# The first expert's rows by fp32 products with the residual, not by a gather

## The chip, the cores and the metric

One Trainium2 chip, one of its cores. The metric is the time of the whole program on the device in microseconds; three runs of the kernel are shown by their median. Engines are named as in the profile: PE is TensorE (PEld its weight loads), DVE VectorE, ACT ScalarE, POOL GpSimd, SP the engine that only issues transfers.

## The reference, cut to what matters

The program runs two transformer layers and then a second block, whose last part is a mixture of 16 experts over 512 tokens of 1024 features:

```python
h = rms_norm_2(x, ffn_norm_gain[i])        # x * rsqrt(mean(x*x) + eps) * gain
x = x + hierarchical_moe(h, ...)

# hierarchical_moe: 4 groups of 4 experts, top-2 experts inside the best group
gates = sum(one_hot(e_glob, N_EXPERTS) * weights[..., None], axis=1)
a = einsum('td,edf->tef', ht, w_e_gate)
u = einsum('td,edf->tef', ht, w_e_up)
hid = silu(a) * u * gates[:, :, None]
out = hid.reshape(t, N_EXPERTS * D_EXPERT) @ w_e_down.reshape(...)   # D_EXPERT = 256
```

## The kernel before

All big products are made of three fp32r products (a high part and a low part of each side, `mm3` and `mm3s`), so each weight tile of 128x2048 is split into a high part on ACT and a low part on DVE before use (`split`, L2004; `whi`, `wlo`).

The class `Moe` does the last part. For each of the four tiles of 128 tokens, `row` (from L1821) transposes the residual `X[t]`, forms the router's logits with eight fp32 products of 20 columns (L1838), gets the norm's factor r by a power on POOL (`rsqrt`, L278), writes the normalised rows `h` to a DRAM tensor `h_rows` (L1841) and the residual to the output (L1842). `route` then picks two experts for each token and gives every chosen token a place, a rank, among the rows of its expert: `rank` (L1892) is a 128x8 tile, one column for each of two choices and four token tiles. `placed` compares the ranks with the slot numbers 0 to 127 (L1899) and sums with small bf16 products (L1909) a table `tab` (L1910): for each expert a list of 128 token numbers, with a number past the end in empty slots. The same is done for the gate weights, `wts`.

`finish` runs 19 slots in order, 16 experts and 3 extra ones for experts with more than 128 tokens. For each slot `gather` (L1977) fetches the 128 rows from `h_rows` by an indirect transfer on POOL's queue into one of three tiles XE, which are the residual tiles `X[0]` to `X[2]`, filled with zeros first (L2071). `rows_in` transposes the rows on PE (L1992), and splits them into a high part on ACT (L1993) and a low part on DVE (L1994), both out of one PSUM tile of two banks. `hidden` makes 24 products with the gate and up weights (L252 to L254), with the next slot's `rows_in` called between its two halves (`between`), then the activation on ACT and the product with the gate weight on DVE (L2024, L2025). `turn` transposes the result (L2032), and `down` multiplies it with the down weights (L260 to L264) and adds the rows to the output by an indirect transfer (L2048). `down` of a slot follows `hidden` of the next one.

Weights come over SP's queue into a ring of 13 buffers (`fetch`, L1811), two transfers in flight at a time; a buffer is free again once `split` has read it. One fetch, the one that is issued when 13 have been sent, also waits for the first gather (`self.first`).

Dependencies and the order of instructions on each engine come from a scheduler of the framework at build time, which follows the program's order as a priority, and takes what is ready by its own timeline. Each engine then works through its list in that order.

Of the kernel before, what the change touches and what calls it, by code (L numbers as in the profile page):

```python
# [10 lines left out]
F32 = mybir.dt.float32  # L11
F32R = mybir.dt.float32r
# [3 lines left out]
AF = mybir.ActivationFunctionType  # L16
ALU = mybir.AluOpType
AX = mybir.AxisListType
SP = mybir.EngineType.SP
P = 128  # L20
D = 1024
KC = 8
# [137 lines left out]
class Kern:  # L160
# [108 lines left out]
                                                                         mybir.DependencyReason.DATA),  # L269
                               reason="side by side")  # L270

    def rsqrt(self, ss, n, dim):

        v = self.nc.vector
        x, y, u = self.tiny(n), self.tiny(n), self.tiny(n)
        v.tensor_scalar(x, ss, 1.0 / dim, EPS, op0=ALU.mult, op1=ALU.add)
        if n <= 4:
            self.nc.gpsimd.tensor_tensor(y, x, self.mhalf[:, :n], op=ALU.pow)  # L278
            return y
        v.tensor_single_scalar(y.bitcast(I32), x.bitcast(I32), 1, op=ALU.logical_shift_right)  # L280
        v.tensor_scalar(y.bitcast(I32), y.bitcast(I32), -1.0, float(0x5F3759DF), op0=ALU.mult, op1=ALU.add)
        for _ in range(3):
            v.tensor_mul(u, y, y)
            v.scalar_tensor_tensor(u, u, -0.5, x, op0=ALU.mult, op1=ALU.mult)
            v.scalar_tensor_tensor(y, u, 1.5, y, op0=ALU.add, op1=ALU.mult)
        return y
# [1450 lines left out]
class Moe:  # L1737
# [4 lines left out]
    def __init__(self, K, out):  # L1742
        self.K, self.out = K, out
        nc, v, gp = K.nc, K.nc.vector, K.nc.gpsimd
# [32 lines left out]
        v.tensor_mul(self.wr, self.wr, K.sm("ffn_gain")[:, :, None].to_broadcast([P, KC, 20]))  # L1777
        self.gain = self.mp.tile([P, D], F32, tag="row", name="ffn_gain")
        nc.scalar.dma_start(self.gain, K.A["ffn_gain"][None, :].to_broadcast([P, D]))
        self.ring = []  # L1780
        self.order = [(0, 0), (0, 1)]
        for e in range(1, 16 + self.EXTRA):
# [12 lines left out]
    def one(self, name, shape, dt=F32):  # L1795
        return self.mp.tile(shape, dt, name=name)
# [24 lines left out]
    def row(self, x, t):  # L1821

        K = self.K
        nc, v = K.nc, K.nc.vector
        d = slice(t * P, t * P + P)
        xT = self.xp.tile([P, KC, P], F32R, tag="xl", name=K.nm("xT")).bitcast(F32)
        b = K.bank2().rearrange("p (k t) -> p k t", k=KC)
        for k in range(KC):
            nc.tensor.transpose(b[:, k, :], x[:, k * P:k * P + P], K.ident)
        for k in (slice(0, 4), slice(4, 8)):  # L1830
            self.turned = nc.scalar.copy(xT[:, k], b[:, k]).ins
        ss = K.tiny(1)
        h = self.xp.tile([P, KC, P], F32R, tag="xh", name=K.nm("h")).bitcast(F32).rearrange("p k t -> p (k t)")
        nc.scalar.activation(h, x, AF.Square, accum_out=ss)
        r = K.rsqrt(ss, 1, D)
        b = K.bank()
        for k in range(KC):
            nc.tensor.matmul(b[:, :20], xT[:, k, :], self.wr[:, k, :], start=k == 0, stop=k == KC - 1)  # L1838
        v.scalar_tensor_tensor(self.lg[:, t, :], b[:, :20], r, K.sm("r_bias"), op0=ALU.mult, op1=ALU.add)
        v.scalar_tensor_tensor(h, x, r, self.gain, op0=ALU.mult, op1=ALU.mult)  # L1840
        nc.gpsimd.dma_start(self.h_d[d, :], h)  # L1841
        nc.gpsimd.dma_start(self.out[d, :], x)  # L1842

    def route(self):
# [45 lines left out]
        tmp4 = tmp.rearrange("p (x t) e -> p x t e", x=2)  # L1890
        v.tensor_mul(tmp4, E4, b[:, :64].rearrange("p (x t e) -> p x t e", x=1, t=4).to_broadcast([P, 2, 4, 16]))
        v.tensor_reduce(rank, tmp, axis=AX.X, op=ALU.add)  # L1892
        cnt, kx, inc, ovb = (one(n, [P, 16]) for n in ("cnt", "kx", "inc", "ovb"))
        v.tensor_copy(cnt, b[:, 64:80])

# [78 lines left out]
    def gather(self, s, xe):  # L1974
# [4 lines left out]
        self.first = self.first or ins  # L1979
        return xe, at  # L1980

    def rows_in(self, pool, xe):

        K = self.K
        nc = K.nc
        if len(self.xs_) < 2:
            self.xs_.append(K.pair(self.xp, "x", [P, KC, P]))
        x = self.xs_[self.nx % 2]
        self.nx += 1
        b = K.bank2().rearrange("p (k t) -> p k t", k=KC)  # L1990
        for k in range(KC):
            nc.tensor.transpose(b[:, k, :], xe[:, k * P:k * P + P], K.ident)  # L1992
        nc.scalar.copy(x[0], b)  # L1993
        nc.vector.tensor_sub(x[1], b, x[0].bitcast(F32))  # L1994
        return x
# [55 lines left out]
    def finish(self, X):  # L2051
# [15 lines left out]
        for i in range(self.NA, self.NA + 5):  # L2067
            self.fetch(i)
        next(r)
        for x in XE:  # L2070
            nc.gpsimd.memset(x, 0.0)  # L2071
        tab = {s: self.gather(s, XE[s]) for s in range(A3)}
        for i in range(self.NA + 5, n1):
            self.fetch(i)
        regs = {}
# [12 lines left out]
            return get  # L2088

        next(r)  # L2090
        x = {0: self.rows_in(pool, tab[0][0])}
        g = {}
        for e in range(N + 1):
            if R <= e <= R + 3:
                next(r, None)
            if e < N:
                if e + A3 < N:
                    tab[e + A3] = self.gather(e + A3, XE[e % A3])

                def rows():  # L2100
                    x[e + 1] = self.rows_in(pool, tab[e + 1][0])
                g[e] = self.hidden(pool, x[e], unit(e), self.wts[:, e:e + 1], rows if e + 1 < N else None)
            if e:
                self.down(g[e - 1], unit(e - 1), Y[e % len(Y)], tab[e - 1][1])
            if e < N:
                g[e] = self.turn(pool, g[e])
# [41 lines left out]
```

## Time and profile before

| what | value |
|---|---|
| median of three runs | 2228.39 us |
| the runs | 2230.19, 2228.39, 2227.59 us |
| the profiled execution | 2229.89 us |
| its span | 2228.2 us |
| granted clock of TensorE, mean | 0.977 |
| PE busy | 2116.9 us |
| DVE busy | 1388.3 us |
| ACT busy | 970.8 us |

The profile is of one execution, and its times count from the start of the span. Busy is the sum of an engine's instructions; a wait is named by what released the engine. The granted clock is the share of 2.4 GHz that PE was given; 0.5 is 1.2 GHz.

### The profile page before, as it was taken

The numbers are of one execution on the slowest core, as the hardware profiler recorded it, in microseconds if no ns is written. First come the engines' busy times: TensorE is split into PE (matmuls) and PEld (weight loads), VectorE is DVE, ScalarE is ACT, GpSimd is POOL, SyncE is SP. The second block draws the span as 40 slices with busy tenths as digits, with TensorE's granted clock in tenths as the row PEclk, the third lists the DMA queues.
The fourth block names the chain that finished last, engine by engine and source line by source line (L and its number), as shares of the span: only waits on it lengthen the run. The fifth ranks groups of instructions, "written<-read, shape, count | busy, mean of one in ns | idle before, by whom it ended". The sixth has DMA issues, their size and how long they took to land. (4 is left out here: it accounts for less than half of the span.)

```text
span 2228.2 us, 28898 instructions
## 1 busy us (share of the span) xinstructions
PE 2116.9 (95%) x11224; PEld 1718.3 (77%) x11224; DVE 1388.3 (62%) x2420; ACT 970.8 (44%) x1484; POOL 327.4 (15%) x457
## 2 busy tenths in 40 slices
PE   6999999999999999999989999999989998997996
PEld 5976668888888888778877888888878875776875
DVE  3666664899744544551694588555646845747875
ACT  5446655521211211451553543222354545635865
POOL 0026632111000000330000100001130000012222
PEclk8999999999999999999999999999999998998998
DMA  7112231557511211121211133424323342668894
GB/s 296 58 38 77 97 142 46 175 186 253 179 58 57 76 57 57 39 92 57 78 57 39 55 110 114 151 91 141 114 92 115 129 143 89 219 256 275 297 307 131
DMA packets 54459, 281.11 MB, mean 126 GB/s; under 512 B 9200, under 2 KB 9600, under 8 KB 29360
## 3 DMA queue, kind: packets, MB, share of 16 engines
q1 hardware_dynamic: 33968, 219.39, 27.6%
q0 software_dynamic: 19344, 57.14, 8.4%
q10 hardware_dynamic: 1008, 2.70, 0.4%
q8 instruction: 90, 1.47, 0.3%
q14 instruction: 49, 0.40, 0.1%
HBM read 266.64 MB, written 26.18 MB: 131 GB/s over the span
## 5 line engine op out<-in xcount | busy, mean ns | idle before, releaser
L233 ACT CAST whi<-raw 128x2048 fp32r<-128x2048 f32 x106 | 202.5, 1911 | 588.9 <-PE b L264 382.8
L234 DVE TENSOR_TENSOR wlo<-raw,whi 128x2048 fp32r<-128x2048 f32 x106 | 246.1, 2323 | 219.4 <-ACT whi L233 217.7
L262 PE MATMUL b<-hl,whi 128*128 128x512 f32 (+1 forms) x736 | 283.2, 385 | 2.6 <-DVE t L335 1.6
L260 PE MATMUL b<-hl,whi 128*128 128x512 f32 (+1 forms) x736 | 282.9, 385 | 1.1 <-ACT whi L233 0.9
L264 PE MATMUL b<-hl,wlo 128*128 128x512 f32 (+1 forms) x736 | 280.5, 385 | 0.0
L833 DVE TENSOR_TENSOR acc<-acc,b 128x512 f32<-128x512 f32 x280 | 180.7, 682 | 147.7 <-PE b L264 147.6
L260 PE MATMUL b<-whi,hid 128*128 128x512 f32 x640 | 213.0, 391 | 3.0 <-ACT whi L233 1.9
L262 PE MATMUL b<-wlo,hid 128*128 128x512 f32 x640 | 214.3, 390 | 0.0
L264 PE MATMUL b<-whi,hid 128*128 128x512 f32 x640 | 211.7, 390 | 0.0
L262 PEld LDWEIGHTS b<-hl,whi 128*128 128x128 f32 x736 | 138.5, 188 | 30.7 <-issue 3.2
L264 PEld LDWEIGHTS b<-hl,wlo 128*128 128x128 f32 x736 | 138.6, 188 | 30.2 <-issue 2.0
L260 PEld LDWEIGHTS b<-hl,whi 128*128 128x128 f32 x736 | 138.4, 188 | 29.6 <-ACT whi L233 1.3
L2004 DVE TENSOR_TENSOR wlo<-raw,whi 128x2048 fp32r<-128x2048 f32 x57 | 129.8, 2288 | 30.8 <-ACT whi L2004 30.8
L260 PEld LDWEIGHTS b<-whi,hid 128*128 128x128 f32 x640 | 118.8, 188 | 27.5 <-ACT whi L233 2.1
L264 PEld LDWEIGHTS b<-whi,hid 128*128 128x128 f32 x640 | 120.1, 188 | 25.6
L262 PEld LDWEIGHTS b<-wlo,hid 128*128 128x128 f32 x640 | 120.1, 188 | 25.0
L2004 ACT CAST whi<-raw 128x2048 fp32r<-128x2048 f32 x57 | 108.2, 1912 | 10.1 <-PE b L254 10.1
L645 POOL TENSOR_TENSOR p<-p,t 128x512 f32<-128x512 f32 (+2 forms) x96 | 92.5, 972 | 63.7 <-DVE t L644 63.3
L414 DVE CUSTOM_DVE_ANT_0 junk<-mw,cb 128x1024 bf16<-128x1024 f32 x80 | 97.6, 1220 | 6.0 <-DMA mw<-in_w_modT_dram 5.4
L641 DVE CUSTOM_DVE_ANT_0 p<-b,mask,nsink 128x512 f32<-128x512 f32 (+2 forms) x96 | 67.4, 704 | 39.2 <-PE b L637 25.7
L643 ACT ACTIVATE p<-p,t 128x513 f32<-128x513 f32 (+2 forms) x96 | 66.2, 690 | 40.3 <-DVE t L644 21.8
L262 PE MATMUL b<-hc,whi 128*128 128x256 f32 x288 | 81.6, 283 | 0.0
(611 smaller groups left out, 4477.6 us busy)
## 6 DMA issues: line engine op xcount, KB each, us to landing
raw<-in_w_e_dram SPq DMA_DIRECT2D x57, 1024.0 KB, 7.4
raw<-in_w_mlp_in_dram SPq DMA_DIRECT2D x32, 1024.0 KB, 5.0
raw<-in_w_mlp_out_dram SPq DMA_DIRECT2D x32, 1024.0 KB, 4.9
mw<-in_w_modT_dram POOLq DMA_DIRECT2D x56, 512.0 KB, 4.6
raw<-in_w_mod_dram SPq DMA_DIRECT2D x20, 1024.0 KB, 7.2
raw<-in_w_in_dram SPq DMA_DIRECT2D x16, 1024.0 KB, 4.9
raw<-in_gla_in_dram SPq DMA_DIRECT2D x12, 1024.0 KB, 4.9
raw<-in_w_o_dram SPq DMA_DIRECT2D x8, 1024.0 KB, 4.9
```

The costliest lines, as they stand in the source:

```text
L233: ins = self.nc.scalar.copy(hi, r).ins
L234: ins = ins, (self.nc.gpsimd if pool else self.nc.vector).tensor_sub(lo, r, hi.bitcast(F32)).ins
L260: mm(o, ah, b, start=start, stop=False)
L262: mm(o, ah, b, start=False, stop=False)
L264: mm(o, al, b, start=False, stop=stop)
L414: v.tensor_tensor_reduce(junk, w, cb[b], 1.0, 0.0, ALU.mult, ALU.add, to[:, k, b:b + 1])
L641: nc.vector.tensor_tensor_reduce(p[:, :n], S[:, a0:a0 + n], added[:, z:z + n], -1.0, ns, ALU.add, ALU.min, nmx)
L643: nc.scalar.activation(p[:, :n + 1], p[:, :n + 1], AF.Exp, bias=nmx, scale=-1.0, accum_out=den)
L645: nc.gpsimd.tensor_mul(p[:, :n], p[:, :n], den.to_broadcast([P, n]))
L833: nc.vector.tensor_add(a, a, bs[n])
L2004: ins = K.nc.scalar.copy(hi, r).ins, K.nc.vector.tensor_sub(lo, r, hi.bitcast(F32)).ins
```

## The change

The normalised rows of slot 0 are computed on the chip from the residual. `rsqrt` gets an argument for its result, so that the factors r of the four token tiles stay in four columns `rn`. In `route`, behind `rank`, two small DVE operations form r8 (rank + 1 where the token's choice is expert 0, else 0) and r0 (the token's slot in expert 0, or -1), and four more form M0: for each token tile a 128x128 matrix that holds r where the slot number equals r0. `first_in` then makes 32 fp32 products, four token tiles times eight feature blocks, of `X[t]` with `M0[t]`, summed over t in one PSUM tile of two banks, which gives slot 0's rows already turned. It reads them out block by block: for each of the eight, ACT writes the high part times the gain, and DVE the low part. In `finish` the gather of slot 0 and the three fills with zeros go, slots 1 to 3 are gathered ahead of the loop into `X[0]` to `X[2]`, and the loop's own gathers start with the second pass. Slot 0 keeps its column of the table for the transfer back.

```diff
--- before.py
+++ after.py
@@ -269,12 +269,13 @@
                                                                          mybir.DependencyReason.DATA),
                                reason="side by side")
 
-    def rsqrt(self, ss, n, dim):
+    def rsqrt(self, ss, n, dim, out=None):
 
         v = self.nc.vector
         x, y, u = self.tiny(n), self.tiny(n), self.tiny(n)
         v.tensor_scalar(x, ss, 1.0 / dim, EPS, op0=ALU.mult, op1=ALU.add)
         if n <= 4:
+            y = y if out is None else out
             self.nc.gpsimd.tensor_tensor(y, x, self.mhalf[:, :n], op=ALU.pow)
             return y
         v.tensor_single_scalar(y.bitcast(I32), x.bitcast(I32), 1, op=ALU.logical_shift_right)
@@ -1777,6 +1778,9 @@
         v.tensor_mul(self.wr, self.wr, K.sm("ffn_gain")[:, :, None].to_broadcast([P, KC, 20]))
         self.gain = self.mp.tile([P, D], F32, tag="row", name="ffn_gain")
         nc.scalar.dma_start(self.gain, K.A["ffn_gain"][None, :].to_broadcast([P, D]))
+
+        self.rn, self.r0, self.r8 = (K.modT[0].rearrange("p a b -> p (a b)")[:, a:a + n]
+                                     for a, n in ((0, 4), (4, 4), (8, 8)))
         self.ring = []
         self.order = [(0, 0), (0, 1)]
         for e in range(1, 16 + self.EXTRA):
@@ -1832,7 +1836,7 @@
         ss = K.tiny(1)
         h = self.xp.tile([P, KC, P], F32R, tag="xh", name=K.nm("h")).bitcast(F32).rearrange("p k t -> p (k t)")
         nc.scalar.activation(h, x, AF.Square, accum_out=ss)
-        r = K.rsqrt(ss, 1, D)
+        r = K.rsqrt(ss, 1, D, self.rn[:, t:t + 1])
         b = K.bank()
         for k in range(KC):
             nc.tensor.matmul(b[:, :20], xT[:, k, :], self.wr[:, k, :], start=k == 0, stop=k == KC - 1)
@@ -1890,6 +1894,13 @@
         tmp4 = tmp.rearrange("p (x t) e -> p x t e", x=2)
         v.tensor_mul(tmp4, E4, b[:, :64].rearrange("p (x t e) -> p x t e", x=1, t=4).to_broadcast([P, 2, 4, 16]))
         v.tensor_reduce(rank, tmp, axis=AX.X, op=ALU.add)
+
+        v.scalar_tensor_tensor(self.r8, rank, 1.0, E[:, :, 0], op0=ALU.add, op1=ALU.mult)
+        v.scalar_tensor_tensor(self.r0, self.r8[:, 0:4], -1.0, self.r8[:, 4:8], op0=ALU.add, op1=ALU.add)
+        self.M0 = self.xp.tile([P, KC, P], F32R, tag="xl", name=K.nm("M0")).bitcast(F32)
+        for t in range(4):
+            v.tensor_scalar(self.M0[:, t, :], self.slots, self.r0[:, t:t + 1], self.rn[:, t:t + 1],
+                            op0=ALU.is_equal, op1=ALU.mult)
         cnt, kx, inc, ovb = (one(n, [P, 16]) for n in ("cnt", "kx", "inc", "ovb"))
         v.tensor_copy(cnt, b[:, 64:80])
 
@@ -1979,6 +1990,25 @@
         self.first = self.first or ins
         return xe, at
 
+    def first_in(self, X):
+
+        K = self.K
+        nc = K.nc
+        x = K.pair(self.xp, "x", [P, KC, P])
+        self.xs_.append(x)
+        self.nx += 1
+        b = K.bank2().rearrange("p (k t) -> p k t", k=KC)
+        for t in range(4):
+            for k in range(KC):
+                nc.tensor.matmul(b[:, k, :], X[t][:, k * P:k * P + P], self.M0[:, t, :], start=t == 0 and k % 4 == 0, stop=t == 3,
+                                 skip_group_check=True)
+        gain = K.sm("ffn_gain")
+        for k in range(KC):
+            nc.scalar.activation(x[0][:, k, :], b[:, k, :], AF.Copy, scale=gain[:, k:k + 1])
+            nc.vector.scalar_tensor_tensor(x[1][:, k, :], b[:, k, :], gain[:, k:k + 1], x[0][:, k, :].bitcast(F32),
+                                           op0=ALU.mult, op1=ALU.subtract)
+        return x
+
     def rows_in(self, pool, xe):
 
         K = self.K
@@ -2067,9 +2097,10 @@
         for i in range(self.NA, self.NA + 5):
             self.fetch(i)
         next(r)
-        for x in XE:
-            nc.gpsimd.memset(x, 0.0)
-        tab = {s: self.gather(s, XE[s]) for s in range(A3)}
+        x = {0: self.first_in(X)}
+        tab = {0: (None, bass.IndirectOffsetOnAxis(ap=self.tab[:, 0:1], axis=0))}
+        for s in range(1, A3 + 1):
+            tab[s] = self.gather(s, XE[s - 1])
         for i in range(self.NA + 5, n1):
             self.fetch(i)
         regs = {}
@@ -2088,14 +2119,13 @@
             return get
 
         next(r)
-        x = {0: self.rows_in(pool, tab[0][0])}
         g = {}
         for e in range(N + 1):
             if R <= e <= R + 3:
                 next(r, None)
             if e < N:
-                if e + A3 < N:
-                    tab[e + A3] = self.gather(e + A3, XE[e % A3])
+                if e and e + A3 < N:
+                    tab[e + A3] = self.gather(e + A3, XE[(e - 1) % A3])
 
                 def rows():
                     x[e + 1] = self.rows_in(pool, tab[e + 1][0])
```

## Rows read from the trace of the kernel before

**Rows 1.** The page, part 1: busy time of the engines.

```profile
PE 2116.9 (95%) x11224; PEld 1718.3 (77%) x11224; DVE 1388.3 (62%) x2420; ACT 970.8 (44%) x1484; POOL 327.4 (15%) x457
```

**Rows 2.** Timeline of PE: start us, us, what, [idle before <-releaser].

```profile
2007.43 0.60 PE L1909 MATMUL b<-oh 128*128 128x16 bf16 x16 [2.22 <-DVE oh L1899]
...
2017.37 3.65 PE L1992 MATMUL b<-ident,x 128*128 128x128 f32 x16 [5.67 <-DMA x<-h_rows,tab]
...
2020.66 0.73 PE L252 MATMUL b<-whi,x 128*128 128x512 f32 x1
...
2026.68 0.39 PE L254 MATMUL b<-whi,x 128*128 128x512 f32 x1
...
2026.91 1.04 PE L1992 MATMUL b<-ident,x 128*128 128x128 f32 x8
...
2029.23 0.47 PE L252 MATMUL b<-whi,x 128*128 128x512 f32 x1
```

**Rows 3.** Windows of PE: stretch, us, busy (instructions), clock, DMA share, GB/s.

```profile
2000.50:2001.00 0.50, 0.14 (x2) 0.72 0.82 213
...
2021.00:2021.50 0.50, 0.50 (x3) 0.80 0.89 320
```

**Rows 4.** Timeline of DVE, 2005 to 2029.

```profile
2005.61 0.28 DVE L1892 TENSOR_REDUCE rank<-rk 128x8 f32<-128x128 f32 x1
...
2006.15 1.22 DVE L1899 TENSOR_TENSOR oh<-slots,rank 128x1024 bf16<-128x1024 bf16 x1
...
2008.10 0.17 DVE L1910 TENSOR_SCALAR tab<-b 128x16 int32<-128x16 f32 x1
...
2026.30 2.29 DVE L2004 TENSOR_TENSOR wlo<-raw,whi 128x2048 fp32r<-128x2048 f32 x1 [2.97 <-ACT whi L2004]
...
2028.50 0.47 DVE L2025 SCALAR_TENSOR_TENSOR g<-g,wts,b 128x256 f32<-128x256 f32 x1
```

**Rows 5.** Timeline of POOL, columns as in rows 2.

```profile
2009.56 1.90 POOL L1977 DMA_INDIRECT x<-h_rows,tab  x1 [8.42 <-DMA raw<-in_w_e_dram]
```

**Rows 6.** DMA issues, 2009.0 to 2010.5: count, median us to landing.

```profile
x<-h_rows,tab POOLq DMA_INDIRECT x1, 7.7
```

**Rows 7.** Waits of SP's queue from 1960 on: us, times, longest.

```profile
SPq L1811 <- DVE wlo L2004: 17.5, 8, 6.0
...
SPq L1811 <- DMA x<-h_rows,tab: 3.2, 1, 3.2
```

**Rows 8.** The instructions of line 1838: ns min/median/max, first and last start.

```profile
L1838 PE MATMUL b<-wr,xT x64: 180/266/287, 1967.9 to 2000.4; 128*128 128x20 f32 x64
```

**Rows 9.** Timeline of PE, an fp32 product in layer 1.

```profile
1135.34 1.06 PE L1068 MATMUL b<-qd,ki 128*128 128x128 f32 x8
```

**Rows 10.** Timeline around a PSUM tile that DVE and ACT read.

```profile
1261.81 1.09 PE L308 MATMUL b<-ident,xn 128*128 128x128 f32 x8 [3.62 <-DVE xn L300]
...
1262.94 1.05 DVE L314 TENSOR_SCALAR h<-b,aff,aff 128x128 f32<-128x128 f32 x3 [1.19 <-PE b L308]
...
1264.10 1.85 ACT L319 ACTIVATE h<-b,aff,aff 128x128 f32<-128x128 f32 x5 [4.02 <-DVE h L314]
```

**Rows 11.** Timeline of ACT and DVE on one SBUF tile.

```profile
49.89 2.93 ACT L518 ACTIVATE xT<-xT,edge_aff,aff 128x512 f32<-128x512 f32 x4 [1.38 <-DVE edge_aff L435]
...
49.97 1.39 DVE L516 TENSOR_SCALAR xT<-xT,aff,edge_aff 128x256 f32<-128x256 f32 x4
```

**Rows 12.** The instructions of line 317, columns as in rows 8.

```profile
L317 ACT ACTIVATE h<-b,small x24: 347/372/396, 1620.4 to 1645.8; 128x128 f32<-128x128 f32 x24
```

**Rows 13.** Timeline of ACT and PE in the routing of one row tile.

```profile
1994.87 1.07 ACT L1831 COPY xT<-b 128x512 f32<-128x512 f32 x2 [1.39 <-PE b L1829]
...
1995.51 1.96 PE L1838 MATMUL b<-wr,xT 128*128 128x20 f32 x16 [0.29 <-ACT xT L1831]
```

**Rows 14.** Timeline of ACT at the end of expert 0.

```profile
2024.36 1.90 ACT L2004 CAST whi<-raw 128x2048 fp32r<-128x2048 f32 x1 [2.29 <-PE b L254]
...
2026.28 1.28 ACT L2024 ACT_TABLE_LOAD   x1
```

## The prediction

> **What bounds the kernel now.** First the page: TensorE (PE) is busy for 95% of the span [rows 1], so a change pays only where PE stands still or works slowly. The one long hole near the change is at the start of the expert loop. Read the PE timeline there [rows 2]: the 16 products that make the slot table start at 2007.43, then PE waits 5.67 us for a gather, and only at 2017.37 come 16 transposes (slots 0 and 1), which take 3.65 us, 0.228 us each; the same transposes cost 1.04/8 = 0.13 us at 2026.91. The windows say why [rows 3]: the granted clock falls from 1.0 to 0.5 (2.4 to 1.2 GHz) in the window at 2000.5, when PE runs dry, and is back in that at 2021.0, some 3.9 us after PE began to work without pause. The first product of expert 0 starts at 2020.66, its last at 2026.68, and expert 1 starts at 2029.23 [rows 2]. Next the wait itself: `rank` is there at 2005.61 + 0.28 = 2005.89, the table at 2008.27 [rows 4]; GpSimd (POOL) starts the first gather at 2009.56 [rows 5], and it lands 7.7 us later, 2017.26 [rows 6]. Last the weight queue: SP waits 17.5 us in eight goes for a buffer that `wlo` has to leave, and 3.2 us for the first gather [rows 7]. So in this stretch the transfers follow PE: a loop that starts earlier pulls them along, one that starts later holds them up.
>
> **The change, part by part.**
>
> *Removed.* Slot 0's gather, and with it the wait that ends at 2017.37; its 8 transposes (half of 3.65 us); three memsets on POOL, which nothing waits for. Of the traffic one gather of 0.52 MB goes; in this stretch, where SP waits for buffers, that is worth nothing on the path.
>
> *Added on VectorE (DVE), behind `rank`.* r8 and r0 by the small row, 0.17 us each, and four 128x128 operations, at most the 0.28 us of the 128x128 reduction that makes `rank` [rows 4]: 0.34 + 1.12 = 1.46 us. The first M0 is there at about 2005.89 + 0.34 + 0.28 = 2006.5; I take 2006.6 with a hand-over. What stands behind them is the 1.22 us comparison for the table [rows 4], so the table comes some 1.4 us later, 2009.7, and later still if its 16 products queue behind others on PE.
>
> *Added on PE: 32 fp32 products.* The code of `row` has 32 fp32 products and the trace 64 instructions [rows 8]: two for each, so 64 come. Eight such of 128 columns took 1.06 us at full clock [rows 9], 0.1325 each. At half clock there is no row of one; from below it is 0.1325, from above double that, and I take the transposes' 0.228, the nearest in shape. The stream starts at 2006.6 at half clock. If the clock rises 3.9 us later, as it did, then 0.6 us go to the table's products [rows 2], 3.3/0.228 = 14 instructions are done, and 50 x 0.1325 = 6.6 us stay, with 0.6 us for the weights' products, taken like the table's: 2006.6 + 3.9 + 6.6 + 0.6 = 2017.7. Bounds: 2006.6 + 64 x 0.1325 + 1.2 = 2016.3 (full clock throughout) and 2006.6 + 64 x 0.228 + 1.2 = 2022.4 (half clock throughout).
>
> *Added: the eviction in sixteen pieces.* This is what I think eats the gain. Where the kernel already lets DVE and ScalarE (ACT) read different parts of one PSUM tile, they go one after the other [rows 10]: eight transposes end at 1262.90, DVE's three pieces start at 1262.94 and take 1.05 us, and ACT, with nothing else named that holds it, starts at 1264.10, 0.11 after DVE's end. The common SBUF tile isn't the reason: in another place both engines write parts of one SBUF tile at the same time [rows 11]. Here each ACT piece is followed by a DVE piece that needs it, and the next ACT piece reads the same PSUM tile. In turns a pair costs 0.372 (ACT, [rows 12]) + 0.35 (DVE, 1.05/3) + two hand-overs of up to 0.11, about 0.9 us; eight are 7.2 us, from 2017.7 to 2024.9. Without turns, eight ACT pieces back to back are at most 8 x 0.372 = 3.0 us.
>
> The Trainium skill (PSUM — Partial Sum Buffer, section "PSUM bank collisions raise a hardware error") speaks against this part: two engines may not touch one bank of the same partitions at once, reads against reads included, and the scheduler orders such a pair. By that rule the eviction takes the 7.2 us; by the other reading of the row (only the tile being written is shared) 3.0 us. The trace agrees with the rule [rows 10, 11], though no row shows sixteen pieces in turn.
>
> *Expert 0.* PE needn't wait for the whole of x: products started after the first half of a copied tile, 0.64 us into a pair of copies that took 1.07 [rows 13]. So expert 0 begins at 2017.7 + 0.9 = 2018.6 instead of 2020.66, and its eight steps of (2026.91 − 2020.66)/8 = 0.78 us, or 0.7 at full clock, follow the pieces. The first four end near 2022.1. Then come slot 1's 8 transposes, 1.04 us. Slot 1's gather needs X[0], free after 16 of the 64 instructions, 2006.6 + 0.6 + 16 x 0.228 = 2010.9, later than the table; with the 7.7 us it lands at 2018.6, in time. The last four steps run from 2023.1 and end at 2025.9: 1.0 us ahead of 2026.91. The fetch that waits for the first gather goes out 1.3 us later than now, which the 17.5 us of waits for buffers hide.
>
> *From expert 0 to expert 1.* Now 2.3 us pass between 2026.91 and 2029.23, and what ends last is g at 2028.50 + 0.47 [rows 2, 4], behind the 2.29 us DVE part of a weight split, which follows its ACT part at 2024.36 and is followed on ACT by a table load of 1.28 us [rows 14]. In the changed kernel ACT is with the eviction until about 2024.5 and then has slot 1's copy, now done long before. If the split still goes first, it starts 1.2 us later (a copy of 1024 columns took 1.07 us in two halves [rows 13]), and expert 1 starts at 2030.4, 1.2 us late. If the activation goes first, the 1.0 us stays. I can't tell the order from here. I take a little better than the middle of −1.0 and +1.2, because the range of the clock's rise is open on the good side too: −0.4 us. From expert 1 on the order of gathers and slots is the old one, and the shift passes through to the end.
>
> **The sum.** The profiled execution took 2229.89 us, 1.7 more than its span, and lies within the runs shown (2227.59 to 2230.19); the shift is set against their median: 2228.39 − 0.4 = 2228.0. The bound for a difference is 0.2%, 4.5 us, about what a measurement of this kernel can tell from no change.
>
> **The rivals.** *(a) No turns:* the eviction overlaps and takes 3.0 us. Expert 0 starts at 2018.4 and PE sets its pace, 8 x 0.7 + 1.04, to 2025.0; ACT is free from about 2020.7, so split and copy are early, and the 1.9 us are kept, or up to 3 with a faster hand-over to expert 1; 2.5 in the middle: 2225.9. For it: eight ACT pieces fit. Against: [rows 10]. *(b) Slower: the table late.* PE takes its queue in order. If the table's 16 products stand behind all 64 instructions, the table comes at 2017.7 + 0.3 + 0.17 = 2018.2, the first gather starts 1.3 us later as now (2008.27 to 2009.56), 2019.5, and lands at 2027.2. Slot 1's transposes stand in the middle of expert 0, so its second half ends at 2027.2 + 1.0 + 2.8 = 2031.0, 4.1 after 2026.91, and the fetch behind the gather goes 10 us late, more than the longest wait for a buffer (6.0, [rows 7]): about +5, 2233.4. It decides once the table's products have more than some 40 instructions ahead of them, where slot 1 lands after 2023. For it: DVE hands M0 over first. Against: the table's products come first in the program, and the trace shows small products woven in where they are ready. *(c) Faster by more:* expert 0 two to three us earlier as in (a), and the earlier stream of weights, less one gather, also takes away waits late in the loop; no row here prices it; twice (a)'s gain is 5.0: 2223.4. *(d) The change doesn't do what it says:* slot 1's transposes stand ahead of expert 0, and its gather replaces slot 0's as the wait: 2018.6 + 1.04 = 2019.6, but the pieces go on meanwhile, and expert 0 still ends at about 2025.9: no other time.
>
> **How the numbers follow.** The forecast, the two shifts cancelling to within 1.5 us, has 0.55, with (d) in it; (a) 0.18; (b) 0.17; (c) 0.10. Faster by over 0.2% is (c), 0.10; slower is (b), 0.17; the rest, 0.73, is no change. The range reaches from 2224.0, which leaves out most of (c), to 2233.5, which takes in (b)'s price but not a longer one. The likeliest case alone lies in 2226.5 to 2229.9.
>
> **What would show it.** Right: 64 PE instructions from about 2006.6 with no wait of 5 us before them; the clock up at about 2010.5; ACT and DVE pieces strictly in turn for about 7 us; expert 0's products from 2018.6; expert 1 within 1.5 us of 2029.23. Wrong: overlapped pieces (then a), the table's products at the end of the stream or slot 1's transposes waiting for a gather after 2021 (then b), or a loop whose order of instructions differs after expert 1.

## The result and the profile after

The changed kernel takes 2240.32 us (median of five runs, 2238.64 to 2246.53); the kernel before took 2228.39 us in the runs beside it (2223.51 to 2230.48). The ratio is 1.0051, 95% interval 1.0034 to 1.0068: 11 to 12 us slower, where 2228.0 was forecast and 2233.5 was the end of the range. The profiled execution shown here took 2240.32 us (span 2238.6).

First a warning on how to compare the two traces. `rank` starts at 2005.61 in the profile before [rows 4] and at 2000.62 in this one, though PE's list of instructions up to there is the same; over the profiles below it lies between 2000.62 and 2011.18. So every time near the change is counted from the start of `rank`. Part 1 of the page after, which answers to [rows 1]:

```profile
PE 2128.5 (95%) x11280; PEld 1728.6 (77%) x11280; DVE 1390.5 (62%) x2433; ACT 973.3 (43%) x1491; POOL 328.1 (15%) x453
```

PE is busy 11.6 us longer than in [rows 1], more than the 9.97 us that the 64 new instructions take below, and its share is still 95%: the page alone doesn't tell where the time went. The PE timeline after, which answers to [rows 2]:

```profile
2002.53 0.59 PE L1920 MATMUL b<-oh 128*128 128x16 bf16 x16 [2.30 <-DVE oh L1910]
2003.54 9.97 PE L2003 MATMUL b<-M,x 128*128 128x128 f32 x64 [0.42 <-DVE M L1902]
...
2013.95 1.07 PE L2022 MATMUL b<-ident,x 128*128 128x128 f32 x8
2014.78 0.48 PE L252 MATMUL b<-whi,x 128*128 128x512 f32 x1
...
2017.39 1.09 PE L2022 MATMUL b<-ident,x 128*128 128x128 f32 x8
...
2021.72 0.50 PE L252 MATMUL b<-whi,x 128*128 128x512 f32 x1 [1.60 <-ACT x L2007]
...
2024.04 0.80 PE L254 MATMUL b<-whi,x 128*128 128x512 f32 x1 [1.59 <-DVE x L2008]
...
2026.77 0.63 PE L254 MATMUL b<-whi,x 128*128 128x512 f32 x1
2030.28 0.69 PE L2062 MATMUL b<-ident,g 128*128 128x128 f32 x2 [2.89 <-DVE g L2055]
2030.62 0.78 PE L252 MATMUL b<-whi,x 128*128 128x512 f32 x1
```

The wait of 5.67 us for the gather is gone, the table's products go ahead of the 64 instructions, and these take 9.97 us without a stop. Slot 1's transposes (2013.95) stand ahead of expert 0 and slot 2's (2017.39) in the middle of it. Expert 0 starts 14.16 us behind `rank`, 0.9 earlier than before (2020.66 − 2005.61 = 15.05). Then it loses: two stops of 1.6 us inside expert 0, each for a piece of the eviction, and one of 2.89 us behind it, for g. Expert 1 starts 30.00 us behind `rank`; before it was 2029.23 − 2005.61 = 23.62. Who keeps the pieces back is seen on ACT and DVE:

```profile
2013.55 0.37 ACT L2007 ACTIVATE x<-b,small 128x128 fp32r<-128x128 f32 x1 [14.33 <-PE b L2003]
...
2015.06 1.01 ACT L2023 CAST x<-b 128x1024 fp32r<-128x1024 f32 x1 [0.36 <-PE b L2022]
...
2019.50 1.90 ACT L2034 CAST whi<-raw 128x2048 fp32r<-128x2048 f32 x1 [0.71 <-PE b L254]
2021.30 0.36 ACT L2007 ACTIVATE x<-b,small 128x128 fp32r<-128x128 f32 x1
2024.02 0.37 ACT L2007 ACTIVATE x<-b,small 128x128 fp32r<-128x128 f32 x1 [2.35 <-DVE x L2008]
...
2027.01 1.01 ACT L2023 CAST x<-b 128x1024 fp32r<-128x1024 f32 x1 [1.83 <-PE b L253]
2028.04 1.28 ACT L2054 ACT_TABLE_LOAD   x1
2029.33 0.39 ACT L2054 ACTIVATE g<-b 128x256 f32<-128x256 f32 x1
```

```profile
2000.62 0.28 DVE L1896 TENSOR_REDUCE rank<-rk 128x8 f32<-128x128 f32 x1
...
2001.26 1.22 DVE L1910 TENSOR_TENSOR oh<-slots,rank 128x1024 bf16<-128x1024 bf16 x1
...
2003.06 1.10 DVE L1902 TENSOR_SCALAR M<-slots,modT 128x128 f32<-128x128 bf16 x4
...
2014.30 1.22 DVE L1910 TENSOR_TENSOR ohx<-slots,q 128x1024 bf16<-128x1024 bf16 x1
...
2016.11 1.23 DVE L2024 TENSOR_TENSOR x<-b,x 128x1024 fp32r<-128x1024 f32 x1
...
2021.43 2.29 DVE L2034 TENSOR_TENSOR wlo<-raw,whi 128x2048 fp32r<-128x2048 f32 x1 [2.26 <-ACT whi L2034]
2023.64 0.34 DVE L2008 SCALAR_TENSOR_TENSOR x<-b,small,x 128x128 fp32r<-128x128 f32 x1
...
2025.20 0.35 DVE L2008 SCALAR_TENSOR_TENSOR x<-b,small,x 128x128 fp32r<-128x128 f32 x1 [0.43 <-ACT x L2007]
```

The sixteen pieces run from 2013.55 to 2025.55: 12.0 us. Between them stand three other pieces of work: the comparison for the extra slots (2014.30), slot 1's copy (2015.06 and 2016.11), and the split of unit (1,1), 1.90 us on ACT and then 2.29 us on DVE (2019.50, 2021.43). (A unit is one weight tile of 128x2048: (e,0) and (e,1) hold the gate and up weights of slot e, (e,2) its down weights.) PE's two stops end with the ACT piece at 2021.30, behind the ACT half of that split, and with the DVE piece at 2023.64, behind its DVE half. Then ACT still has slot 2's copy, which waits for the products of expert 0 to end, and a table load ahead of the activation that g needs. What PE's clock did meanwhile, in windows with the columns of [rows 3] (PE, PEld, DVE, ACT, POOL, then clock, DMA share, GB/s):

```profile
2017.20:2020.60 3.40, 2.85 (x16) 2.07 (x15) 1.10 (x4) 1.84 (x3) 0.99 (x1) 1.00 0.73 231
2020.70:2024.10 3.40, 0.79 (x3) 0.36 (x3) 2.56 (x2) 1.05 (x3) 0.00 (x0) 0.78 0.58 236
2024.10:2027.50 3.40, 3.29 (x7) 2.08 (x7) 0.70 (x2) 1.15 (x3) 0.00 (x0) 0.50 0.83 272
```

The granted clock is 1.0 up to the first stop, falls behind it to 0.5 (0.78 is the mean of the second window), and stays there through the third stop until 2036.3. A product then starts every 0.43 us, not every 0.23: the last seven of expert 0 and the first thirteen of expert 1. Two rows of before that were not shown yet, of PE and of POOL, and the first scatter after (a scatter is the indirect transfer that adds a slot's rows to the output):

```profile
2029.03 0.44 PE L2032 MATMUL b<-ident,g 128*128 128x128 f32 x2 [1.08 <-DVE g L2025]
```

```profile
2040.73 1.65 POOL L2048 DMA_INDIRECT out_dram<-xy,tab  x1 [0.30 <-issue]
```

```profile
2044.76 3.74 POOL L2078 DMA_INDIRECT out_dram<-xy,tab  x1 [0.30 <-ACT whi L2034]
```

So the first scatter comes 44.14 us behind `rank` instead of 35.12, 9.0 late, and that adds up: −0.9 at the start of expert 0; +3.2 by the two stops; +1.5 by seven products at half clock (2024.04 to 2027.2 is 3.16 us, and 7 x 0.233 would be 1.63); +0.85 by the eight transposes at 2017.39, which stood in the hand-over before, where PE waited anyway; +1.8 by the stop for g (2.89 against 1.08); and +2.6 in expert 1 (its interval is 12.50 us against 9.89; thirteen products at 0.2 us more).

### The profile page after: what moved, and what is told of

Same layout as the page of the kernel before. It is cut to its first block, busy times and chain, and to the rows that moved or that the text cites. A ratio compares the mean times of both kernels' runs of the same rounds, so it can differ in the third digit from the quotient of the medians.

```text
span 2238.6 us, 29024 instructions
## 1 busy us (share of the span) xinstructions
PE 2128.5 (95%) x11280; PEld 1728.6 (77%) x11280; DVE 1390.5 (62%) x2433; ACT 973.3 (43%) x1491; POOL 328.1 (15%) x453
## 5 line engine op out<-in xcount | busy, mean ns | idle before, releaser
L642 DVE CUSTOM_DVE_ANT_0 p<-b,mask,nsink 128x512 f32<-128x512 f32 (+2 forms) x96 | 67.5, 704 | 39.0 <-PE b L638 25.7
```

The source lines that it names most:

```text
L642: nc.vector.tensor_tensor_reduce(p[:, :n], S[:, a0:a0 + n], added[:, z:z + n], -1.0, ns, ALU.add, ALU.min, nmx)
```

## The experiments

Three theories stood against each other. **1**: the eviction in turns, with other work let in between its pieces, makes the loop start late, by stops and by the clock that falls with them. **2**: the 64 fp32 instructions, at half clock and behind a late M0, are what costs. **3**: the loop is slower for another reason. All runs in one table; the two starts are from the traces, counted from `rank`; "slot 18" is the time from PE's first product of the last slot to PE's last product of all; the ratio is to the kernel before on the same chip (medians 2228.0 to 2230.0), and the last column is (ratio − 1) x 2229 with its interval. The ratio isn't the quotient of the medians, which gives up to 2.5 us more or less. Edits are shown shortened.

| run | expert 1 | first scatter | slot 18 | median us | ratio | us above before |
|---|---|---|---|---|---|---|
| before | 23.6 | 35.1 | 13.0 | | | |
| changed | 30.0 | 44.1 | 16.7 | 2240.32 | 1.0051 | 11.4 (7.6 to 15.2) |
| changed, again | 28.6 | 42.5 | 16.7 | 2241.97 | 1.0060 | 13.4 (9.4 to 17.4) |
| pieces alone | 28.5 | 41.9 | 15.1 | 2240.47 | 1.0061 | 13.6 (8.5 to 18.7) |
| products alone | 26.3 | 37.9 | 13.0 | 2229.61 | 1.0013 | 2.9 (−0.2 to 6.0) |
| two loops | 23.2 | 34.7 | 13.0 | 2228.85 | 1.0009 | 2.0 (−1.6 to 5.8) |
| three operations | 25.7 | 38.7 | 16.7 | 2237.04 | 1.0040 | 8.9 (4.2 to 13.4) |
| held copies | 25.7 | 38.8 | 15.1 | 2237.02 | 1.0037 | 8.2 (4.5 to 11.8) |
| delay | 29.3 | 40.9 | 13.0 | 2234.73 | 1.0030 | 6.7 (3.6 to 9.6) |
| two loops, four orders | 21.3 | 32.1 | 13.0 | 2228.22 | 0.9998 | −0.4 (−3.1 to 2.5) |
| before, late order of changed | 23.4 | 34.9 | 14.9 | 2231.07 | 1.0006 | 1.3 (−0.7 to 3.3) |
| two loops, late order of changed | 23.0 | 34.6 | 14.8 | 2230.60 | 1.0001 | 0.2 (−3.3 to 4.0) |
| changed, late order of before | 29.9 | 44.0 | 13.0 | 2239.48 | 1.0037 | 8.2 (4.9 to 11.6) |
| held, late order of before | 24.6 | 38.6 | 13.0 | 2234.34 | 1.0021 | 4.7 (1.6 to 7.6) |
| pieces alone, late order of before | 30.4 | 44.4 | 13.0 | 2236.50 | 1.0023 | 5.1 (1.8 to 8.7) |
| four orders and before's whole loop order | 21.3 | 32.1 | 13.0 | 2230.14 | 0.9994 | −1.3 (−4.7 to 2.0) |

**Pieces alone.** One part of the change in the kernel before: slot 0 by gather and transposes as ever, its copy and subtraction in sixteen pieces.

```diff
-        nc.scalar.copy(x[0], b)                       # slot 0 only
-        nc.vector.tensor_sub(x[1], b, x[0].bitcast(F32))
+        for k in range(KC):
+            nc.scalar.activation(x[0][:, k, :], b[:, k, :], AF.Copy, scale=one[:, k:k + 1])
+            nc.vector.scalar_tensor_tensor(x[1][:, k, :], b[:, k, :], one[:, k:k + 1], x[0][:, k, :]...
```

> The kernel before, gather and transposes kept, with only slot 0's copy and subtraction made in the 16 pieces of the change (scale 1). Theory 1: the pieces start at about 2019.6, take 8 to 12 us in turns, mixed with slot 1's copy; expert 1 starts 3 to 8 us later than in the kernel before, and the time is 3 to 9 us above it. Theories 2 and 3: within 3 us of the kernel before.

Measured: 13.6 us above, somewhat over theory 1's 9, and as much as the whole change. PE's timeline has stops like those of the changed kernel:

```profile
2026.08 0.50 PE L252 MATMUL b<-whi,x 128*128 128x512 f32 x1 [0.90 <-ACT x L1999]
...
2028.40 0.50 PE L254 MATMUL b<-whi,x 128*128 128x512 f32 x1 [1.60 <-DVE x L2000]
...
2032.85 0.69 PE L2039 MATMUL b<-ident,g 128*128 128x128 f32 x2 [3.08 <-DVE g L2032]
```

**Products alone.** The other part alone: M0 and 64 fp32 instructions ahead of the transposes, into a tile that nobody reads.

```diff
+        for t in range(4):
+            v.tensor_scalar(self.M0[:, t, :], self.slots, rank[:, t:t + 1], rank[:, t + 4:t + 5],
+                            op0=ALU.is_equal, op1=ALU.mult)
+        self.unused(X[3])            # 32 fp32 products with M0
         x = {0: self.rows_in(pool, tab[0][0])}
```

> The kernel before, with its gather, transposes and whole-tile copies, and in addition the M0 operations and 64 fp32 instructions of the change, all on the fourth block of the residual and into a PSUM tile that nobody reads (their result is not used; rank's columns stand in for r0 and rn). Theory 1: the products run in the wait for the gather and end about 12.5 us behind the start of rank, so expert 1 starts 23 to 25 us behind rank as in the kernel before, and the time is within 3 us of it. Theory 2 (the products are what costs): 8 us or more above.

Measured: 2.9 us, the interval touches zero. The start was expected 23 to 25 us behind `rank` and came at 26.3: here 26 of the 64 stand ahead of the table's products, the gather goes out later, and PE waits 1.58 and 1.73 us for two of them. That is the prediction's rival (b) in small, and not what happened in the changed kernel. With these two runs theory 2 falls as the main cause.

**Two loops.** All pieces of ACT are issued ahead of all pieces of DVE.

```diff
         for k in range(KC):
             nc.scalar.activation(x[0][:, k, :], b[:, k, :], AF.Copy, scale=gain[:, k:k + 1])
+        for k in range(KC):
             nc.vector.scalar_tensor_tensor(x[1][:, k, :], b[:, k, :], gain[:, k:k + 1], ...
```

> The changed kernel with all eight ScalarE pieces of the eviction issued ahead of all eight VectorE pieces, so that no piece of the one waits for the piece before it of the other. Theory 1: 8 x 0.37 and then 8 x 0.35 us, 6 to 7 us from the last product to the last piece, no weight split between them; expert 1 starts 24 to 27 us behind rank, and the time is 0 to 4 us above the kernel before. Theory 2 or 3: 8 to 12 us above, as the changed kernel.

Measured: 2.0 us, the loss is gone. The pieces take 4.4 us instead of the expected 6 to 7, and expert 1 starts 23.2 us behind `rank`, ahead of the expected 24. ACT and DVE in this run, and PE behind expert 0:

```profile
2016.61 2.17 ACT L2007 ACTIVATE x<-b,small 128x128 fp32r<-128x128 f32 x8 [14.38 <-PE b L2003]
```

```profile
2018.82 2.16 DVE L2009 SCALAR_TENSOR_TENSOR x<-b,small,x 128x128 fp32r<-128x128 f32 x8
```

```profile
2026.58 0.44 PE L2063 MATMUL b<-ident,g 128*128 128x128 f32 x2 [1.09 <-DVE g L2056]
```

Eight pieces in a row take 2.17 us on ACT and 2.16 us on DVE, 4.4 us from the first to the last instead of 12.0; the stop for g is 1.09 us as before, and the clock stays up in expert 1. The scheduler also put slot 2's copy behind the activation here and kept the late order of before (see below), so this run doesn't tell the length of the eviction from the orders that came with it.

**Held copies.** The turns stay; slot 1's copy and the split of unit (1,1) are ordered behind the last piece.

```diff
-        if self.nhi == 3:
-            for i, a in zip(ins, (self.turned, self.placed)):
+        if self.nhi in (3, 4):
+            for i, a in zip(ins, (self.turned, self.placed) if self.nhi == 3 else self.evicted):
```

> The changed kernel with its 16 pieces as they are, but slot 1's copy and the weight split of unit (1,1) ordered behind the last piece on both engines. If what stands between the pieces is what costs (first half of theory 1): the turns take 8 x 0.78 = 6.3 us and one VectorE comparison more, about 8 us; expert 0 has no stop of 1.6 us, but the split comes later and g behind it, so expert 1 starts 25 to 28 us behind rank, and the time is 2 to 6 us above the kernel before. If the turns alone cost (second half of theory 1), or by theories 2 and 3: 8 to 12 us above.

Measured: 8.2 us, over the 2 to 6 that the first half of theory 1 had, and inside the 8 to 12 of its second half; expert 1 starts at 25.7, inside the first half's 25 to 28. ACT's first and last piece, DVE's last, and the stop for g:

```profile
2021.50 0.37 ACT L2007 ACTIVATE x<-b,small 128x128 fp32r<-128x128 f32 x1 [14.47 <-PE b L2003]
...
2028.08 0.37 ACT L2007 ACTIVATE x<-b,small 128x128 fp32r<-128x128 f32 x1 [0.42 <-DVE x L2008]
```

```profile
2028.48 0.35 DVE L2008 SCALAR_TENSOR_TENSOR x<-b,small,x 128x128 fp32r<-128x128 f32 x1 [0.43 <-ACT x L2007]
```

```profile
2033.92 0.53 PE L2066 MATMUL b<-ident,g 128*128 128x128 f32 x2 [3.58 <-DVE g L2059]
```

The turns take 2021.50 to 2028.83, 7.3 us, of which one VectorE comparison between the first two pairs takes 1.1; PE no longer stops 1.6 us for a piece. But copy, split, table load and activation now queue behind them on ACT, PE waits 3.58 us for g, and the first products of expert 1 again start every 0.43 us. So of the 6.4 us by which expert 1 starts late in the changed kernel, 4.3 go with the copy and the split between the pieces; 2.1 stay, with the length of the turns and with what now stands behind them. This run doesn't part those two.

**Three operations.** DVE multiplies the whole tile by the gain, ACT copies, DVE subtracts.

```diff
-        (sixteen pieces)
+        nc.vector.tensor_mul(xf, b, gain[:, :, None].to_broadcast([P, KC, P]))
+        nc.scalar.copy(x[0], xf)
+        nc.vector.tensor_sub(x[1], xf, x[0].bitcast(F32))
```

> The changed kernel with the eviction of the products in three operations on the whole 128x1024 tile (VectorE times the gain into an own SBUF tile, ScalarE copies the high part, VectorE subtracts) in place of 16 pieces. Theory 1 (what costs is the eviction in turns, with other copies and a weight split let in between its pieces): about 1.2 + 1.0 + 1.2 us and at most 2 us of other VectorE work in between, so x is complete some 5.5 us behind the last product instead of 12; expert 0 runs without a stop longer than 1 us, expert 1 starts 23 to 26 us behind the start of rank (before 23.6, changed 30.0), and the time is within 4 us of the kernel before. Theory 2 (the 64 fp32 instructions at half clock behind a late M0 are what costs): nothing of that changes, so 8 to 12 us above the kernel before. Theory 3 (the loop is slower for another reason, such as the order of gathers and slots): expert 1 may start early, and the time is still 8 us or more above.

Expert 1 starts 25.7 us behind `rank`, inside theory 1's 23 to 26, and PE stops for the eviction only once, 0.88 us ahead of the first product; the time, 8.9 us above, misses the 4 that theory 1 gave. The scheduler put slot 2's copy and its subtraction ahead of the activation and of g, as in the changed kernel, and PE waits for g:

```profile
2025.64 1.22 DVE L2024 TENSOR_TENSOR x<-b,x 128x1024 fp32r<-128x1024 f32 x1
2026.80 0.48 DVE L2055 SCALAR_TENSOR_TENSOR g<-g,wts,b 128x256 f32<-128x256 f32 x1
```

```profile
2027.34 0.69 PE L2062 MATMUL b<-ident,g 128*128 128x128 f32 x2 [3.08 <-DVE g L2055]
```

A short eviction doesn't help by itself: what stands on ACT and DVE behind it decides.

**Delay.** Twice the unused products, a late start with PE at work and the hand-over as before.

```diff
-        for t in range(4):
+        for t in range(8):           # in unused(), M0[t % 4]
```

> As the run with unused products, but with twice as many (128 instructions): a start of the loop that is late with TensorE working all the time, its clock up and the hand-over to expert 1 as before. They end some 19 us behind rank instead of 12.5, so expert 0 and expert 1 start 5 to 7 us later than in the kernel before. If a late start passes through to the end one to one, as the prediction had it: 5 to 7 us above the kernel before. If the loop gives some back: under 3 us. If a late start of this size costs a further 4 us in the loop, as the runs with three operations and with the held copies suggest (3.6 us late by the profile, 8 in the time): 9 to 12 us.

Expert 1 starts 5.7 us late, the stop for g is 1.09 us, and the time is 6.7 us above, inside the 5 to 7 of one to one: a late start passes to the end about one to one. But in the runs of theory 1 the time is 2 to 7 us more than the first scatter is late: 8.2 and 8.9 for 3.6, 13.6 for 6.7, 11.4 and 13.4 for 9.0 and 7.4. The changed kernel once more, for its spread:

> The changed kernel once more, unaltered, on the chip of the three others, for a second profile. Theory 1: again stops of 1.5 us and more inside expert 0 and some 3 us behind it, expert 1 28 to 31 us behind rank, first scatter 8 to 10 us later by rank than in the kernel before, 10 to 14 us above it in time. Theory 3: the start differs from profile to profile by more than 3 us with the same time.

Its start repeats within 1.6 us of the first profile, with the stops, and so does its time.

**The late order.** The lists of instructions show what these runs share. Late in the loop before, two loops, products alone and delay have one order on ACT and DVE; changed, pieces alone, held copies and three operations have another, at three places: the split of unit (16,0) stands behind the Silu of slot 15, that of (17,1) behind slot 18's copy, that of (18,1) behind the copy into Y for slot 16 (Y is the tile from which a scatter goes). The third place in the changed kernel, on ACT and on PE, and then on ACT with the order of before forced on it:

```profile
2210.62 1.02 ACT L2077 COPY xy<-b 128x1024 f32<-128x1024 f32 x1 [2.36 <-PE b L264]
2211.53 1.91 ACT L2034 CAST whi<-raw 128x2048 fp32r<-128x2048 f32 x1
```

```profile
2215.82 0.50 PE L253 MATMUL b<-wlo,x 128*128 128x512 f32 x1 [1.82 <-DVE wlo L2034]
```

```profile
2212.54 1.90 ACT L2040 CAST whi<-raw 128x2048 fp32r<-128x2048 f32 x1
...
2215.22 1.02 ACT L2084 COPY xy<-b 128x1024 f32<-128x1024 f32 x1 [0.78 <-PE b L264]
```

ACT waits 2.36 us for what it copies into Y, the split behind it comes late, and PE stops 1.82 us for that unit's low part; with the split first, there is no such stop. Theory **4** was that this order makes the excess.

The edit orders three pairs without a wait; the kernel before gets the order of the changed one, and the other way round.

```diff
+        self.order_late([("S15", "W47"), ("X18", "W51"), ("Y16", "W54")])     # in before: as in changed
+        self.order_late([("W47", "S15"), ("W51", "X17"), ("W54", "Y16")])     # in changed: as in before
```

> The kernel before with nothing of the change, except that ScalarE and VectorE have the changed kernel's order at three places late in the loop (the split of unit (16,0) behind the Silu of slot 15, that of (17,1) behind slot 18's copy, that of (18,1) behind the copy into Y for slot 16). Theory 4 (the excess of some 4 us over the late start comes from this late order, which the change brought along): 3 to 6 us above the kernel before, with the start of the loop as in it. If the excess is a later effect of the late start, or chance: within 2 us of the kernel before.

> The changed kernel with the order of the kernel before at the same three places. Theory 4: the start stays 7 to 9 us late, and the time is 7 to 10 us above the kernel before instead of 12 to 14. Otherwise: 11 to 14 us above.

> The run with the held copies (expert 1 starting 2.1, the first scatter 3.7 us late, 8 us in the time) with the order of the kernel before at the same three places. Theory 4: 3 to 5 us above the kernel before. Otherwise: 7 to 9 us above, as it was.

> The run with the 16 pieces in the kernel before (first scatter 6.7 us late, 13.6 us above by the ratio, late order as in the changed kernel), with the late order of the kernel before at the three places. If the late order costs 3 to 4 us wherever the loop starts late: 8 to 11 us above the kernel before. If not: 12 to 15 us above.

> The run with the two loops (start as in the kernel before, 2.0 us above it by the ratio), with the late order of the changed kernel at the three places. If the late order costs 3 to 4 us by itself: 5 to 6 us above the kernel before. If it costs that only where the loop starts late: 1 to 3 us above.

Where the loop starts late, the order of before takes 3 to 5 us off the changed kernel (8.2 against 11.4 and 13.4), 3.5 off held copies, 8.5 off pieces alone (by the medians 1.4 to 4.6); 8.2 and 4.7 lie where theory 4 had them. The intervals overlap in each pair, but all three point one way, and with this order four late starts of 3.5, 5.7, 8.9 and 9.3 us cost 4.7, 6.7, 8.2 and 5.1 us. Pieces alone with that order came in below the expected 8 to 11. Where the loop doesn't start late, the times show nothing (1.3 and, from 2.0, 0.2); for the kernel before, theory 4 as it was written had 3 to 6.

The traces are sharper than the times. Slot 18 takes PE 13.0 us in all nine profiles with the split of (18,1) first, and 14.8 to 16.7 in all seven with it behind the copy, also where the loop starts on time (14.9 and 14.8). So the third place costs 1.8 to 3.7 us by itself, which the intervals of those two runs (up to 3.3 and 4.0) allow; for the other two places no cost is shown. The lateness of the first scatter and this loss in slot 18 add up: 9.0 + 3.7 = 12.7 and 7.4 + 3.6 = 11.0 for the two profiles of the changed kernel (measured 11.4 and 13.4), and for 14 of the 15 runs of the table the sum lies in the interval. Pieces alone with the order of before is the one that doesn't fit (9.3, interval to 8.7). The rule was found in these profiles, one for each run, and not forecast.

**A version with the best of all.** Two loops, and four orders: M0 ahead of the table's comparison, the second comparison behind the pieces, a small unread Silu that loads the table early, the DVE half of the split of (1,1) behind g.

```diff
+        a.activation(one("early", [P, 4]), e2, AF.Silu)
+            self.behind_on_dve(cmp, m0 if name == "oh" else self.evicted, "first rows first")
+        if self.nhi == 4:
+            self.behind_on_dve(ins[1], self.g0, "g first")
```

> The changed kernel with the two loops of the eviction and four orders more: M0 ahead of the table's comparison, the second comparison behind the last piece, the Silu table loaded early by a small Silu that nobody reads, and VectorE's part of the split of unit (1,1) behind g of expert 0. Theory 1: M0 1 us earlier, pieces up to 1.5 us earlier, 0.5 to 1 us less between expert 0 and expert 1: expert 1 starts 20 to 22 us behind rank (before 23.6), and the time is 1 to 4 us below the kernel before. If the start of the loop doesn't set the time: within 2 us of the run with the two loops alone.

> The run with the two loops and four orders more (first scatter 3 us earlier than in the kernel before, and no time gained; its order of the loop differs from that of the kernel before in a dozen places), with the order of the kernel before on ScalarE and VectorE from the Silu of slot 0 to the end. If it was the order that took the gain: 2 to 4 us below the kernel before. If an earlier start gives nothing because something later sets the end: within 1 us of it.

```profile
2005.64 4.59 PE L2008 MATMUL b<-M,x 128*128 128x128 f32 x26 [2.18 <-DVE M L1902]
...
2017.28 1.07 PE L2029 MATMUL b<-ident,x 128*128 128x128 f32 x8 [1.73 <-DMA x<-h_rows,tab]
...
2024.94 0.44 PE L2072 MATMUL b<-ident,g 128*128 128x128 f32 x2
...
2161.03 0.73 PE L260 MATMUL b<-whi,g 128*128 128x512 f32 x2 [3.08 <-ACT whi L2041]
```

```profile
2157.89 1.01 ACT L2087 COPY xy<-b 128x1024 f32<-128x1024 f32 x1 [6.18 <-DMA out_dram<-xy,tab]
...
2159.07 1.91 ACT L2041 CAST whi<-raw 128x2048 fp32r<-128x2048 f32 x1
```

The stop for g is gone, expert 1 starts 2.3 us and the first scatter 3.0 us earlier than before. The time isn't lower beyond its interval (−0.4, and −1.3 with before's order in the whole loop; the intervals reach −3.1 and −4.7, so 3 us aren't excluded). The second is within 1 us of the first, as expected if something later sets the end. PE now waits for slot 1's gather instead (1.73 us). Where the lead goes can be followed in the profile of the first: by `rank`, PE is 5.0 us ahead of the kernel before at the first product of slot 14, and 0.5 behind at that of slot 15. In between, ACT waits 6.18 us for a scatter to land before it can fill Y anew, the split behind it is late, and PE stops 3.08 us for it. In all 16 profiles the scatters go one after the other: from the third to the fifteenth, each starts 0.8 to 1.6 us behind the landing of the one before. From the start of the first to the landing of the fourteenth this chain takes 149.8 us before, 152.6 and 156.8 in these two runs, 143.9 to 156.8 over all. A lead of 3 us is less than this spread; what makes a scatter longer or shorter is not shown. No version beats the kernel before by what can be measured.

## Why the prediction was wrong

**The step that failed** is the eviction with what follows it: "eight are 7.2 us", "the last four steps run from 2023.1 and end at 2025.9", and "I take a little better than the middle of −1.0 and +1.2 [...]: −0.4 us". That −0.4 is the one shift in the sum; expert 1 came 6.4 us late by `rank` (30.00 − 23.62; 5.0 in the second profile), and the late order, which no term had, adds 3.7 in slot 18.

- *M0 and the products.* M0 was predicted 1.0 us behind the start of `rank` and the first product came 2.9 behind it, since DVE took the table's comparison first. The 64 instructions took 9.97 us, and the prediction's 14 at 0.228 and 50 at 0.1325 make 9.8, but that is luck: the clock rose 5.4 us behind the first of them instead of 3.9, so 25 ran at half clock, and one took less than assumed at either clock (0.213 and 0.112 us from start to start). The table's products went first, so rival (b) didn't happen. Slot 1's transposes stood ahead of expert 0, as in rival (d) and not in its middle; (d) put no cost on it, but slot 1's copy came among the pieces that way.
- *The turns* were right: strictly alternating, 0.785 us for a pair against 0.9. The Trainium skill (PSUM — Partial Sum Buffer, section "PSUM bank collisions raise a hardware error") has two engines never at once on one bank; the traces agree, the next piece always waiting for the other engine's (0.42 and 0.43 us in the held run). The order that was built holds for the whole tile: ACT's fifth piece, the first in the second bank, waits for DVE's fourth like the rest. No run here shows what would happen without that order. By themselves eight pairs are 6.3 us; the 7.3 of held copies, near the predicted 7.2, has a comparison in it. In the changed kernel it was 12.0: the prediction asked what each piece waits for, and not what else the scheduler would put between sixteen pieces on two engines that had copies and a split ready.
- *The hand-over.* Even with clean turns expert 1 starts 2.1 us late, beyond the bound of 1.2, as slot 1's copy, a split and the table load stand between the last piece and g. In the changed kernel it is 6.4.
- *The clock* was counted for its rise only. It falls again with the stops, and the products behind it cost 1.5 us in expert 0 and 2.6 in expert 1. No term had that.
- *"The shift passes through to the end"* holds (delay run: 5.7 late, 6.7 in the time). *"The order of gathers and slots is the old one"* was true of gathers and slots, not of ACT and DVE late in the loop; the prediction named such a difference as a sign of error. It costs 3.7 us in slot 18 of the changed kernel. "The transfers follow PE" was read from waits of SP's queue without the greatest of that view, 157.5 us in 47 goes for weight transfers in flight, and the scatters, which go one behind the other, were not in the sum at all.
- *Rival (a)* is not what two loops show: ACT's and DVE's pieces don't overlap there either, the turns are only fewer. It gives the start of before, and not the 2.5 us.

## What to carry to other kernels

A PSUM tile that two engines read in turn costs a hand-over for each piece, and each hand-over is a gap into which a scheduler puts other work: issue all pieces of one engine and then all of the other, and look at what stands behind them on both. Removing a wait pays only as far as the next waits allow; here g and slot 1's rows were next in the same stage, and a chain of scatters later. A stop costs TensorE twice where the clock falls with it. And an edit at one place can change a built order some 180 us later: compare the lists of instructions before the time is put down to the edit.

## What the runs showed of the hardware

- Where pieces stand back to back, one of 128x128 takes ACT 2.17/8 = 0.27 us and DVE 0.27 us; the next starts 0.1 us ahead of the end of the one before, as a single piece lasts 0.37 and 0.35 us. In turns there is no such overlap, and the pair takes 0.785.
- A stop of 1.1 us for g left the granted clock at 1.0 (two loops, delay). Stops of 3.08 and 3.58 us (three operations, held copies) were followed by 0.5. A stop of 1.82 us was followed by 0.5 in slot 18 of the changed kernel and late in the delay run, and by none in slot 18 of held copies.
- The scatters, each behind the landing of the one before, took 5.2 to 14.4 us each beside the weight transfers (the first thirteen of every profile).
- The same instructions ahead of `rank` bring it at 2000.6 to 2011.2 us in these profiles, a spread as large as the effect: a difference of 0.5% needed many runs and times counted from a common point.
